# Block inverses of 16 as leading pieces in a two-layer hybrid encoder, with all projections as fill

## The chip, the cores and the metric

The kernel runs on one core of one Trainium2 chip. The metric is the device time of one execution in microseconds (us). TensorE (PE) multiplies matrices, VectorE (DVE), ScalarE (ACT) and GpSimd (POOL) work element by element, and SyncE (SP) issues most transfers. Each engine works through its own instructions in the order in which they stand in the program and waits for semaphores where it needs another engine's result.

## The reference, cut to what matters

Two layers over 512 tokens of width 1024, in float32. Each layer has a mixer and then a mixture of 16 experts:

```
xn = rmsnorm(x);  proj = xn @ w_in
y_a = gmlp_spatial_gating(a_u, a_v, ...)             # chunks of 128 tokens
y_b = dilated_attention(b_q, b_k, b_v, positions)    # 6 heads, q/k norm + rotary
y_c = gated_deltanet(c_qkv, c_gate, c_a, c_b, ...)   # 6 heads, forward and backward scan
x = x + concat(y_a, y_b, y_c) @ w_out
x = x + expert_choice_ffn(rmsnorm(x)) ; x = x + rmsnorm(p @ w_ple) * sigmoid(...)
# inside gated_deltanet, per chunk:
t_inv = triangular_solve(lower + eye, eye)           # unit lower triangular
u = t_inv @ (v * beta);  w = t_inv @ (k * beta * exp(g))
# then a scan: v_new = u - w @ state;  o = q @ state + qk @ v_new;  state = ...
```

The kernel uses chunks of 32 tokens, so it inverts 2 directions x 96 triangles of 32 x 32 per layer (24 column groups on each of 4 groups of 32 partitions, for each direction).

## The kernel before

The change is in the mixer of each layer (0 to 440 us in layer 0, 960 to 1390 us in layer 1). The experts behind it keep PE nearly full and are not touched.

The float32 products are three matmuls each (`mm3`, L345: high part by high part, low by high, high by low), so every weight is first split: `wnext` (L319) lets ACT make the rounded high part `whi` (L338) and POOL the remainder `wlo` (L340). In `mixer` (L371) the order of the code is: the projection and convolution for the DeltaNet (`gdn_qkv`; its PSUM tile is `cq`, its DVE tiles `acc` and `sl`, its transposes `tokp`), the chunks' Gram matrices (`gdn_chunk`, `pG`, `AT`), the inverse (`gdn_inv`, L883), the end of the gating (`gmlp_out`, L582: `mixp`, `ya`, `yap`), the rotary tables in layer 0, the attention's projection of q and k (`attn_qk`, L472), the transposed inverse (`gdn_inv_T`, L905), and then the scan over 16 chunks (`gdn_scan`, L915) interleaved with the rest of the attention and with the first part of the output projection.

`gdn_inv` does 30 steps on DVE, each of one product `T` (L900) and one sum into `X` (L902), over the rows below the step, for both directions at once. `gdn_inv_T` transposes `X` into `XT` by two DVE instructions and multiplies by beta (L911, L912). The first product of the scan (`pV`, L951) reads `XT`.

`attn_qk` has three groups i of 256 columns and four token tiles t. `first(i)` does 24 `mm3` matmuls into `qkp` for each t, copies and squares them on ACT, then computes the norm's factor `ra` on DVE (L183 to L190, 13 small operations), multiplies on POOL (L530) and rotates on DVE (L535 to L538). `second(i, t)` transposes the result on PE (`qkTp`, L504) and copies it on ACT into `att`. The transposes of group i are emitted behind the projections of group i + 1.

Two things set the order. The framework's scheduler places the instructions of the mixer's first part on each engine freely, by its own priorities. From the scan on `interleave` (L454) works: the scan is the lead, cut into pieces by `yield`, and the rest of the attention and the output projection (`w_out_first`) are the fill. Each lead piece yields a number, which is paid off with fill pieces; `in_order` (L435) pins the order of the pieces on PE by letting a piece issue after the last PE instruction of the piece before. The other engines are not pinned: a fill piece's work on DVE, ACT and POOL can go ahead of the lead's. `INIT` fill pieces come first; `FILLS` are the numbers that the scan yields.

Of the kernel before, what the change touches and what calls it, by code (L numbers as in the profile page):

```python
# [38 lines left out]

OWED = 0.5  # L40

INIT = 3
FILLS = (1.9, 1.5, 1.1)

QKV_BLOCKS = ((4, 5), (2, 3), (0, 1), (6, 7), (8,))
# [72 lines left out]
class K:  # L118
# [252 lines left out]
    def mixer(self, l):  # L371
        nc, tc, A = self.nc, self.tc, self.A
        with tc.tile_pool(name=f"mix{l}", bufs=1, reuse_waits="tile") as mp:
            self.mp = self.sm = mp
            self.t = lambda i, shape, name: mp.tile(shape, F32, tag=f"t{i}", name=name, bufs=2)
            self.p1 = lambda shape, name: mp.tile(shape, F32, tag="p1", name=name, bufs=3)
            self.p2 = lambda shape, name: mp.tile(shape, F32, tag="p2", name=name, bufs=2)
            self.one = lambda shape, name: mp.tile(shape, F32, tag=name, name=name, bufs=1)

            for tag, n, bufs in (("qk", 1024, 2), ("amask", S + 384, 1), ("wsT", 512, 1), ("mcst", CROUTE - CKEEP, 1),  # L380
                                 ("p1", 512, 3), ("p2", 512, 2)):
                for _ in range(bufs):
# [12 lines left out]
            specs += [(wo[0:640, c:c + n], n, 5) for c, n in WO_COLS]  # L395
            specs += [(wo[640:1024, 512 * i:512 * i + 512], 512, 3) for i in range(2)]
            self.wplan(specs)
            wuv = [self.wnext()]
            if l == 0:
                self.load_x(range(1, NT))  # L400
            xs = self.gslot("xs").rearrange("p (t d) -> p t d", t=2)
            tv = lambda name: self.slot(name).rearrange("p (k n) -> p k n", k=4)
            self.xh, self.xl = [tv("xh") for _ in range(2)], [tv("xl") for _ in range(2)]
            for t in range(NT):
                if t == 2:
                    wuv.append(self.wnext(pieces=4))
                self.norm(t, g, xs[:, t % 2, :])
                self.norm_T(t, xs[:, t % 2, :], self.xh, self.xl)
            self.setup2(l)
            self.gmlp(l, wuv)  # L410
            self.gate_decay(l)

            qkv = self.gdn_qkv(l)
            next(qkv)
            self.gdn_chunk(l)
            wq = self.wnext(ahead=False)
            next(qkv, None)
            self.gdn_inv(l)
# [12 lines left out]
            self.wo2 = [self.wnext() for _ in range(2)]  # L431
            self.gdn_out(l)
        self.w_out_last(l)

    def in_order(self):  # L435

        last = None

        def piece(gen):
            nonlocal last  # L440
            with ExitStack() as st:
# [3 lines left out]
            ins = self.nc.cur_bb.bb.instructions  # L445
            k = len(ins) - 1
            while ins[k] is not last and ins[k].engine != self.nc.tensor.engine:
                k -= 1
            last = ins[k]
            return r  # L450

        return piece

    def interleave(self, lead, fill):  # L454


        piece, owed = self.in_order(), 0.0
        for _ in range(INIT):
            piece(fill)
        while True:  # L460
            r = piece(lead)
            if r is None:
                return
            owed += r
            while owed > OWED:
                r = piece(fill)
                if r is None:
                    break
                owed -= r


    def attn_qk(self, l, wq):  # L472
# [41 lines left out]
        def first(i, w):  # L514
# [25 lines left out]

        self.wload(small=True)
        for i in range(3):
            first(i, self.wnext(small=True) if i else wq)
        self.qk_rest = lambda: second(*late.pop(0)) if late else None


# [35 lines left out]
    def gmlp_out(self, l):  # L582
# [6 lines left out]
        for j in range(2):  # L589
            self.mark("gmlp")  # L590
            ya = self.p1([128, NT, 128], "ya")
            for i in range(2):
                g = 2 * j + i
                p = self.pc([128, NT, 64], "mixp")
                pe.matmul(p, wsT[:, g, :], uv[:, :, 256 + g * 64:256 + g * 64 + 64], start=True, stop=True)
                v.scalar_tensor_tensor(ya[:, :, i * 64:(i + 1) * 64], p, bs[:, g:g + 1],
                                       uv[:, :, g * 64:(g + 1) * 64], op0=ALU.add, op1=ALU.mult)
            pt = self.pc([128, NT, 128], "yap")
            for t in range(NT):
                pe.transpose(pt[:, t, :], ya[:, t, :], self.ident)  # L600
            self.split(self.yTa[0][:, j, :], self.yTa[1][:, j, :], pt.rearrange("p t c -> p (t c)"), 0.5)

    def attn_v(self, l, wv):
        self.mark("attn_v")
        for t in range(NT):
            p = self.pb([128, 384], "vp")
            for i in range(2):
# [275 lines left out]
    def gdn_inv(self, l):  # L883
# [5 lines left out]
        v.transpose(brT, br)  # L889
        v.tensor_scalar(brT, brT, -1.0, None, op0=ALU.mult)  # L890
        X = self.gslot("X").rearrange("p (c i j) -> p c i j", c=2, i=32)
        for dr in range(2):
            Xd = X[:, dr] if dr == 0 else X[:, dr].rearrange("p i j -> p j i")
            v.transpose(Xd, AT[:, dr].rearrange("p m b -> p b m"))
            v.tensor_tensor(Xd, Xd, brT[:, dr, :, None].to_broadcast([128, 32, 32]), op=ALU.mult)
        pool_e.memset(X.rearrange("p c i j -> p c (i j)")[:, :, ::33], 1.0)
        for j in range(1, 31):
            n = 31 - j
            T = self.t(3, [128, 2, n, j], "T")
            v.tensor_tensor(T, X[:, :, j + 1:, j:j + 1].to_broadcast([128, 2, n, j]),  # L900
                            X[:, :, j:j + 1, 0:j].to_broadcast([128, 2, n, j]), op=ALU.mult)
            v.tensor_tensor(X[:, :, j + 1:, 0:j], X[:, :, j + 1:, 0:j], T, op=ALU.add)  # L902
        self.X = X

    def gdn_inv_T(self, l):  # L905
        self.mark("invT")
        v, pe, br, X = self.nc.vector, self.nc.tensor, self.br, self.X
        XT = self.XT = self.gslot("XT").rearrange("p (d m b) -> p d m b", d=2, m=32)
        for dr in range(2):
            Xd = X[:, dr] if dr == 0 else X[:, dr].rearrange("p i j -> p j i")  # L910
            v.transpose(XT[:, dr].rearrange("p m t -> p t m"), Xd)  # L911
        v.tensor_tensor(XT[:, :, 0:24], XT[:, :, 0:24], br[:, :, 0:24, None].to_broadcast([128, 2, 24, 32]), op=ALU.mult)  # L912


    def gdn_scan(self, l):  # L915
# [588 lines left out]
```

## Time and profile before

| | us |
|---|---|
| median of 3 runs | 1958.14 (1953.76 to 1958.29) |
| the profiled execution | 1962.08 |
| its span | 1960.3 |
| PE busy in the span | 1809.5 (92%) |
| DVE busy | 931.7 (48%) |
| ACT busy | 523.9 (27%) |
| POOL busy | 457.4 (23%) |

The profile is of one execution. In the windows view a row has the stretch in us, its length, and then for PE, PEld (PE's weight loads), DVE, ACT and POOL the busy time and in brackets the instructions; the last three numbers are the clock that TensorE was granted (1.00 is 2.4 GHz, 0.50 is 1.2 GHz), the share of the DMA engines and GB/s. In the timeline a row has the start, the time, the engine, the line, the operation, what it writes and reads, its tile sizes, and how many instructions were drawn together; in brackets the engine's idle time ahead of it and the instruction whose end released it. A float32 matmul or transpose through PE stands in the trace as two instructions; in the order listings below it is one. Line numbers of the kernel after are higher than those of before by up to 50.

### The profile page before, as it was taken

To read this page: it belongs to the slowest core of one execution; us is meant where nothing else is said; L and a number is where in the kernel's file an instruction comes from. 1 tells how busy PE (TensorE), PEld (TensorE's weight loads), DVE (VectorE), ACT (ScalarE), POOL (GpSimd) and SP (SyncE) were. 2 spreads that over 40 slices of the span, in tenths; PEclk is the share of its full clock that TensorE was granted. 3 is DMA by queue.
4 is the path that set the end of the run, shared out by engine and by line. 5 is a ranking of instruction groups with operands and counts; after the bars stand their busy time and mean duration, and the time that the engine had idled before them with its cause. 6 is when DMAs were issued, how large, how long until landed. Compare 5 with 4: busy or idle time off the path is not lost.

```text
span 1960.3 us, 30038 instructions
## 1 busy us (share of the span) xinstructions
PE 1809.5 (92%) x12216; PEld 1140.4 (58%) x12216; DVE 931.7 (48%) x2088; ACT 523.9 (27%) x1213; POOL 457.4 (23%) x402
## 2 busy tenths in 40 slices
PE   6898698979999999999989978899799999999999
PEld 5777665864344444434988767568544344443358
DVE  5879767671112121132778796776511212114126
ACT  4334444331010101102443344552311011011023
POOL 3544313320000003021645452233100000031025
PEclk9998788989999999999998977999799999999999
DMA  5212020187799999899342020202987999998991
GB/s 169 86 33 60 17 85 15 56 329 302 321 423 421 409 421 407 345 412 379 111 134 76 24 74 2 97 2 102 411 321 318 422 421 397 422 394 345 380 328 66
DMA packets 122394, 467.47 MB, mean 238 GB/s; under 512 B 11664, under 2 KB 68496, under 8 KB 75920
## 3 DMA queue, kind: packets, MB, share of 16 engines
q1 hardware_dynamic: 115168, 458.46, 59.5%
q10 hardware_dynamic: 7088, 7.09, 1.2%
q8 instruction: 96, 1.57, 0.3%
q14 instruction: 42, 0.34, 0.1%
HBM read 461.32 MB, written 4.19 MB: 237 GB/s over the span
## 4 chain that ended last, share of the span: by engine, by line
PE 69%; DVE 20%; ACT 3%; issue 3%; POOL 2%; DMA 2%; ACTq 0%; SPq 0%; DVEq 0%; POOLq 0%
PE pGt L1276 14%; PE pUp L1276 11%; PE pY L1276 10%; DVE acc L778 3%; PE xep L1206 2%; PE ysc L1295 2%; DVE rr L944 2%; PE xep L1207 2%; PE pY L1391 2%; PE pV L951 1%; PE op L348 1%; PE ysc L1296 1%; PE pgp L348 1%; PE pgp L350 1%; PE plep L1172 1%
## 5 line engine op out<-in xcount | busy, mean ns | idle before, releaser
L1276 PE MATMUL pGt<-w,xe 128*64 128x512 f32 x592 | 194.8, 607 | 0.0
L340 POOL TENSOR_TENSOR wlo<-w,whi 128x512 fp32r<-128x512 f32 (+5 forms) x66 | 162.1, 2473 | 102.9 <-ACT whi L338 71.9
L1276 PE MATMUL pUp<-w,xe 128*64 128x512 f32 x688 | 178.4, 593 | 0.0
L1343 POOL TENSOR_TENSOR x<-x,hh 128x1024 f32<-128x1024 f32 x8 | 18.8, 2356 | 620.0 <-DMA wx<-in_w_e_up_dram 310.4
L1276 PE MATMUL pY<-w,hidT 128*64 128x512 f32 x608 | 162.5, 596 | 0.2 <-ACT hidT L1350 0.2
L1360 DVE SCALAR_TENSOR_TENSOR yl<-pY,gsl,yh 128x512 fp32r<-128x512 f32 x28 | 21.0, 751 | 203.1 <-ACT yh L1359 201.5
L1301 DVE TENSOR_TENSOR x<-ysc,x 128x512 f32<-128x512 f32 x96 | 62.9, 686 | 110.5 <-PE ysc L1296 110.5
L1276 PEld LDWEIGHTS pUp<-w,xe 128*64 128x64 f32 x688 | 62.9, 137 | 89.5 <-issue 86.3
L1276 PEld LDWEIGHTS pGt<-w,xe 128*64 128x64 f32 x592 | 56.1, 137 | 99.2 <-issue 92.7
L1276 PE MATMUL pGt<-wx,xe 128*64 128x512 f32 x384 | 113.0, 599 | 0.3
L1334 DVE SCALAR_TENSOR_TENSOR hid<-sg,gsl,pUp 128x512 f32<-128x512 f32 x32 | 23.9, 748 | 169.8 <-PE pUp L1276 168.0
L1276 PEld LDWEIGHTS pY<-w,hidT 128*64 128x64 f32 x608 | 55.6, 136 | 76.2 <-issue 73.3
L1276 PE MATMUL pUp<-wx,xe 128*64 128x512 f32 x320 | 99.8, 595 | 0.0
L1276 PE MATMUL pY<-wx,hidT 128*64 128x512 f32 x288 | 86.2, 595 | 0.0
L1327 DVE SCALAR_TENSOR_TENSOR sg<-sg,pGt 128x512 f32<-128x512 f32 x32 | 21.7, 686 | 131.3 <-ACT sg L1326 131.3
L338 ACT ACTIVATE whi<-w 128x512 fp32r<-128x512 f32 (+5 forms) x66 | 68.2, 1058 | 38.5 <-PE op L349 15.8
L1326 ACT ACTIVATE sg<-pGt,gsl 128x512 f32<-128x512 f32 x32 | 21.8, 687 | 196.5 <-PE pGt L1276 194.6
L1350 ACT ACTIVATE hidT<-htp 128x512 f32<-128x512 f32 x32 | 19.0, 597 | 200.4 <-PE htp L1349 200.4
L1206 PE MATMUL xep<-OH,hh 128*128 128x256 f32 x256 | 70.1, 307 | 2.4 <-DVE OH L1194 2.4
L778 DVE SCALAR_TENSOR_TENSOR acc<-raw,pp,acc 128x512 f32<-128x512 f32 x72 | 64.3, 894 | 15.5 <-ACT acc L776 13.0
L348 PE MATMUL pgp<-whi,gTh 128*128 128x256 f32 x256 | 70.9, 281 | 0.0
L350 PE MATMUL pgp<-whi,gTl 128*128 128x256 f32 x256 | 69.8, 282 | 0.3 <-DVE gTl L279 0.3
(404 smaller groups left out, 4277.3 us busy)
## 6 DMA issues: line engine op xcount, KB each, us to landing
w<-in_w_e_up_dram SPq DMA_DIRECT2D x86, 1024.0 KB, 15.4
w<-in_w_e_down_dram SPq DMA_DIRECT2D x76, 1024.0 KB, 12.7
w<-in_w_e_gate_dram SPq DMA_DIRECT2D x74, 1024.0 KB, 15.6
wx<-in_w_e_gate_dram SPq DMA_DIRECT2D x48, 1024.0 KB, 9.9
wx<-in_w_e_up_dram SPq DMA_DIRECT2D x40, 1024.0 KB, 16.7
wx<-in_w_e_down_dram SPq DMA_DIRECT2D x36, 1024.0 KB, 12.0
wd<-in_w_e_down_dram SPq DMA_DIRECT2D x32, 512.0 KB, 8.3
w<-in_w_in_dram SPq DMA_DIRECT2D x14, 1024.0 KB, 5.2
```

The source lines that it names most:

```text
L338: self.nc.scalar.activation(rr_(hi[:, ks, :]), wk, AF.Copy)
L340: e.tensor_tensor(rr_(lo[:, ks, :]), wk, hi[:, ks, :], op=ALU.subtract)
L348: pe.matmul(p, lh, rh, start=first, stop=False)
L350: pe.matmul(p, ll, rh, start=False, stop=last)
L778: v.scalar_tensor_tensor(acc, raw[:, kk:kk + S], conv[:, b, kk:kk + 1], acc, op0=ALU.mult, op1=ALU.add)
L944: v.tensor_tensor(rr[kl[dr], :], vtok[kl[dr], tl, :], fl(tm[kl[dr]]), op=ALU.subtract)
L1206: pe.matmul(p, rr_(hh[:, t, ks]), OHf[:, t, :], start=(t == 0), stop=False)
L1207: pe.matmul(p, rr_(hl[:, t, ks]), OHf[:, t, :], start=False, stop=(t == NT - 1))
L1276: pe.matmul(pt[nh][64 * ei:64 * ei + 64, :], lhs[:, kk, 64 * ei:64 * ei + 64], wt[ei][k][:, nh * 512:nh * 512 + 512], start=(kk == 0), sto ...
L1295: pe.matmul(p, rr_(OT[:, t, :]), rr_(yh[:, ns]), start=True, stop=False)
L1301: v.tensor_tensor(xv, p, xv, op=ALU.add)
L1391: pe.matmul(pY[64 * ei:64 * ei + 64, :], hidT[:, 4 * half + k, 64 * ei:64 * ei + 64], wt[ei][:, k, :], start=(half + k == 0), stop=(half * ...
```

## The change

The inverse now works on four blocks of 16 x 16 (two per direction and triangle) in a new tile `XN`, by 14 steps in place of 30. The block off the diagonal of each 32 x 32 triangle comes from two products on PE: `pY1` (`AT` by `XN`) and, after a multiplication by beta on DVE (`Y`), `pY2` (`Y` by `XT`), which DVE subtracts in `XT`. ACT copies the blocks into `X`, POOL sets zeros and ones. There are two more transposes on DVE for it.

The inverse, its transposition and the scan are now one lead; the end of the gating, the projections of q, k and v, the attention and the first part of the output projection are one fill, with `yield`s added. A projection of one t and the transposes that it carries are in one piece. `in_order` also lets a fill piece's DVE, ACT and POOL instructions issue only behind the last instruction of the lead on that engine. `INIT` is 1.

```
-INIT = 3
+INIT = 1
...
-            self.gdn_inv(l)
-            self.gmlp_out(l)
-            if l == 0:
-                self.trig()
-            nc.scalar.dma_start(self.amask, A["amask"])
-            self.attn_qk(l, wq)
-            self.gdn_inv_T(l)
-            wv = [self.wnext(small=True), self.wnext()]
-
-            other = chain(self.attn_v(l, wv), self.core(l), self.w_out_first(l))
-            self.interleave(self.gdn_scan(l), other)
+
+            other = chain(self.gmlp_out(l), self.attn_qk(l, wq), self.attn_v(l), self.core(l), self.w_out_first(l))
+            self.interleave(chain(self.gdn_inv(l), self.gdn_inv_T(l), self.gdn_scan(l)), other)
...
+                if not leads:
+                    for i in ahead.values():
+                        st.enter_context(self.tc.issue_after(i))
                 r = next(gen, None)
...
+                elif leads and i.engine in (self.nc.vector.engine, self.nc.scalar.engine, self.nc.gpsimd.engine):
+                    ahead[i.engine] = i
...
-            r = piece(lead)
+            r = piece(lead, True)
...
                 if late:
                     second(*late.pop(0))
+                yield 2.6
...
+        XN = self.XN = self.one([128, 2048], "XN")
+        B = XN[:, 0:1024].rearrange("p (c e i j) -> p c e i j", c=2, e=2, i=16)
...
-        for j in range(1, 31):
-            n = 31 - j
-            T = self.t(3, [128, 2, n, j], "T")
...
+        yield 5.0
+        for j in range(1, 15):
+            n = 15 - j
+            T = self.t(3, [128, 4, n, j], "T")
+            v.tensor_tensor(T, Bf[:, :, j + 1:, j:j + 1].to_broadcast([128, 4, n, j]),
+                            Bf[:, :, j:j + 1, 0:j].to_broadcast([128, 4, n, j]), op=ALU.mult)
+            v.tensor_tensor(Bf[:, :, j + 1:, 0:j], Bf[:, :, j + 1:, 0:j], T, op=ALU.add)
+            if j % 2 == 0:
+                yield 2.6
+        for i in range(2):
+            s = slice(16 * i, 16 * i + 16)
+            act.activation(X[:, :, s, s], B[:, :, i], AF.Copy)
...
+        for dr in range(2):
+            v.transpose(flip(XN[:, dr]), flip(X[:, dr]) if dr == 0 else X[:, dr])
+        yield 6.0
+        for dr in range(2):
+            p = self.pg([128, 24, 16], "pY1")
+            for m in range(24):
+                for r in rows:
+                    pe.matmul(p[r, m, :], AT[r, dr, m, :], XN[r, dr, m, cs[dr][0]], start=True, stop=True)
+            v.tensor_tensor(Y[:, dr, :, cs[dr][0]], p, br[:, dr, 0:24, None].to_broadcast([128, 24, 16]), op=ALU.mult)
+        for dr in range(2):
+            v.transpose(flip(XT[:, dr]), X[:, dr] if dr == 0 else flip(X[:, dr]))
+        yield 5.0
+        for dr in range(2):
+            p = self.pg([128, 24, 16], "pY2")
+            for m in range(24):
+                for r in rows:
+                    pe.matmul(p[r, m, :], Y[r, dr, m, :], XT[r, dr, m, cs[dr][1]], start=True, stop=True)
+            xo = XT[:, dr, 0:24, cs[dr][1]]
+            v.tensor_tensor(xo, xo, p, op=ALU.subtract)
+            xd = XT[:, dr, 0:24]
+            v.tensor_tensor(xd, xd, br[:, dr, 0:24, None].to_broadcast([128, 24, 32]), op=ALU.mult)
+        yield 4.0
```

On PE, in layer 0, right behind the last projection of the DeltaNet (`cq`), before:

```order
L349 MATMUL cq_1350<-xl_102,whl_1113 128x512
L350 MATMUL cq_1350<-xh_100,whl_1113 128x512
L348 MATMUL qkp_1587<-whi_1301,xh_99 128x256
L349 MATMUL qkp_1587<-wlo_1302,xh_99 128x256
L350 MATMUL qkp_1587<-whi_1301,xl_101 128x256
L348 MATMUL qkp_1587<-whi_1301,xh_99 128x256
L349 MATMUL qkp_1587<-wlo_1302,xh_99 128x256
```

and after, at the same place:

```order
L349 MATMUL cq_1350<-xl_102,whl_1113 128x512
L350 MATMUL cq_1350<-xh_100,whl_1113 128x512
L807 MATMUL tokp_1389<-cst_64,sl_1342 128x128 x4
L807 MATMUL tokp_1395<-cst_64,sl_1387 128x128 x4
L596 MATMUL mixp_1407<-uv_239,wsT_237 128x256
L596 MATMUL mixp_1410<-uv_239,wsT_237 128x256
L601 MATMUL yap_1413<-cst_64,ya_1406 128x128 x4
L596 MATMUL mixp_1435<-uv_239,wsT_237 128x256
L596 MATMUL mixp_1438<-uv_239,wsT_237 128x256
L601 MATMUL yap_1441<-cst_64,ya_1434 128x128 x4
L348 MATMUL qkp_1502<-whi_1301,xh_99 128x256
L349 MATMUL qkp_1502<-wlo_1302,xh_99 128x256
```

Before, 96 matmuls `qkp` of the first group stand ahead of the second `tokp`; after, none does, and all of them stand behind the last `yap`.

The first transpose `qkTp` of q and k (`qk_1584` before, `qk_1499` after, the rotated first group), on PE in layer 0, before:

```order
L348 MATMUL qkp_1959<-whi_1938,xh_100 128x256
L349 MATMUL qkp_1959<-wlo_1939,xh_100 128x256
L350 MATMUL qkp_1959<-whi_1938,xl_102 128x256
L504 MATMUL qkTp_1788<-cst_64,qk_1584 128x128 x2
L504 MATMUL qkTp_1826<-cst_64,qk_1584 128x128 x2
L348 MATMUL qkp_1996<-whi_1938,xh_99 128x256
```

and after:

```order
L348 MATMUL qkp_1690<-whi_1669,xh_100 128x256
L349 MATMUL qkp_1690<-wlo_1670,xh_100 128x256
L350 MATMUL qkp_1690<-whi_1669,xl_102 128x256
L504 MATMUL qkTp_1721<-cst_64,qk_1499 128x128 x2
L348 MATMUL qkp_1734<-whi_1669,xh_99 128x256
L349 MATMUL qkp_1734<-wlo_1670,xh_99 128x256
```

Before, 216 matmuls `qkp` stand ahead of it: all of groups 0 and 1 and the first t of group 2; after, 120 do: group 0 and the first t of group 1. From there on a pair of transposes follows each t, so that the first pair of group 1 stands behind the first t of group 2. `pY1` stands behind the seventh pair, `pY2` behind the eighth and six `vp`.

On POOL, in the scan of layer 0 (`St` is the state's decay of one step, `o_sum` the output's sum in steps 8 to 15, `wlo` of 128x1920 and 128x1280 a low part for `w_out_first`), before:

```order
L961 TENSOR_TENSOR St<-St,ex 128x384 x5
L340 TENSOR_TENSOR wlo<-w,whi 128x1920
L961 TENSOR_TENSOR St<-St,ex 128x384 x2
L340 TENSOR_TENSOR wlo<-w,whi 128x1920
L961 TENSOR_TENSOR St<-St,ex 128x384 x2
L988 TENSOR_TENSOR o_sum<-tmp,o_sum 32x384 x2
```

and after, from the tenth step on:

```order
L1037 TENSOR_TENSOR o_sum<-tmp,o_sum 32x384 x2
L340 TENSOR_TENSOR wlo<-w,whi 128x1920
L1010 TENSOR_TENSOR St<-St,ex 128x384
L1037 TENSOR_TENSOR o_sum<-tmp,o_sum 32x384 x2
L1010 TENSOR_TENSOR St<-St,ex 128x384
L1037 TENSOR_TENSOR o_sum<-tmp,o_sum 32x384 x4
L340 TENSOR_TENSOR wlo<-w,whi 128x1920
L340 TENSOR_TENSOR wlo<-w,whi 128x1280
```

The first two low parts stood behind the decays of steps 5 and 7; now they stand behind `o_sum` of steps 11 and 14, and on PE the first output matmul that reads each of them stands right behind: behind `pV` of step 12 and behind `pO` of step 14.

## Rows read from the trace of the kernel before

**Rows 1.** Windows: the stage ahead of the scan and the scan, both layers.

```profile
154.00:228.00 74.00, 52.12 (x346) 47.90 (x344) 71.96 (x131) 37.73 (x157) 32.48 (x35) 0.82 0.19 50
...
228.00:382.00 154.00, 141.63 (x1988) 105.77 (x1989) 99.87 (x277) 61.79 (x143) 43.63 (x36) 0.89 0.11 38
...
1120.00:1196.00 76.00, 57.17 (x379) 51.65 (x377) 74.15 (x143) 37.47 (x157) 33.30 (x35) 0.80 0.19 49
1196.00:1347.00 151.00, 137.75 (x1989) 103.22 (x1990) 100.43 (x277) 62.10 (x144) 43.60 (x36) 0.92 0.12 38
```

**Rows 2.** Lines of DVE, 154 to 228: busy, mean ns, idle before.

```profile
L902 DVE TENSOR_TENSOR X<-X,T 128x60 f32<-128x60 f32 (+14 forms) x30 | 24.6, 821 | 0.4
L900 DVE TENSOR_TENSOR T<-X 128x60 f32<-128x60 f32 (+14 forms) x30 | 18.4, 613 | 0.4
...
L911 DVE STREAM_TRANSPOSE XT<-X 128x1024 f32<-128x1024 f32 x2 | 4.1, 2140 | 0.0
```

**Rows 3.** Waits of PE, 154 to 228: total us, times, longest.

```profile
PE qkTp L504 <- DVE qk L538: 11.6, 1, 11.6
```

**Rows 4.** Timeline of PE, layer 0, from `cq` to the transposes.

```profile
154.16 0.27 PE L348 MATMUL qkp<-whi,xh 128*128 128x256 f32 x1
...
168.79 0.66 PE L801 MATMUL tokp<-cst,sl 128*128 128x128 f32 x4 [2.22 <-DVE sl L783]
...
178.53 0.58 PE L349 MATMUL qkp<-wlo,xh 128*128 128x256 f32 x1 [0.96 <-POOL wlo L340]
...
195.06 0.28 PE L350 MATMUL qkp<-whi,xl 128*128 128x256 f32 x1
```

**Rows 5.** Timeline of ACT, DVE and POOL: from a projection to its rotation.

```profile
175.66 0.24 ACT L524 ACTIVATE sqa<-qk 128x64 f32<-128x64 f32 x1
...
197.79 3.95 POOL L530 TENSOR_TENSOR qk<-qk,ra 128x256 f32<-128x256 f32 x4 [9.73 <-DVE ra L190]
...
201.77 4.06 DVE L535 TENSOR_TENSOR ro<-qk,rot 128x128 f32<-128x128 f32 x4 [0.50 <-POOL qk L530]
...
215.91 2.96 POOL L530 TENSOR_TENSOR qk<-qk,ra 128x256 f32<-128x256 f32 x4 [10.22 <-DVE ra L190]
...
228.06 0.16 DVE L183 TENSOR_SCALAR nr<-ssq 128x16 f32<-128x16 f32 x1
...
230.43 0.17 DVE L190 SCALAR_TENSOR_TENSOR ra<-nr,ra 128x16 f32<-128x16 f32 x1
...
236.04 0.90 DVE L535 TENSOR_TENSOR ro<-qk,rot 128x128 f32<-128x128 f32 x4
```

**Rows 6.** Timeline of PE: small matmuls by tiles of 32.

```profile
148.15 0.77 PE L875 MATMUL pG<-KQT 64*32 64x64 f32 x48
...
361.11 0.86 PE L951 MATMUL pV<-rr,XT 32*32 32x64 f32 x24
```

**Rows 7.** Timeline of PE, DVE, POOL and ACT in the scan of layer 0.

```profile
258.48 0.85 PE L951 MATMUL pV<-rr,XT 32*32 32x64 f32 x22 [0.22 <-DVE rr L944]
...
267.26 0.85 PE L951 MATMUL pV<-rr,XT 32*32 32x64 f32 x22 [0.23 <-DVE rr L944]
...
271.89 1.81 ACT L338 ACTIVATE whi<-w 128x1920 fp32r<-128x1920 f32 x1
...
273.77 4.24 POOL L340 TENSOR_TENSOR wlo<-w,whi 128x1920 fp32r<-128x1920 f32 x1 [0.35 <-ACT whi L338]
...
275.14 3.86 DVE L944 TENSOR_TENSOR rr<-vtok,tm 32x384 f32<-32x384 f32 x2
...
279.06 1.30 PE L951 MATMUL pV<-rr,XT 32*32 32x64 f32 x22 [0.22 <-DVE rr L944]
...
299.07 5.05 DVE L944 TENSOR_TENSOR rr<-vtok,tm 32x384 f32<-32x384 f32 x2
...
316.68 0.92 PE L951 MATMUL pV<-rr,XT 32*32 32x64 f32 x24
...
321.84 2.14 POOL L988 TENSOR_TENSOR o_sum<-tmp,o_sum 32x384 f32<-32x384 f32 x2
```

More of the change, by code (lines that the diff above doesn't have):

```diff
@@ L435, in in_order, with piece @@
     def in_order(self):
-        last = None
-        def piece(gen):
+        last, ahead = None, {}
+        def piece(gen, leads=False):
             nonlocal last
+            ins = self.nc.cur_bb.bb.instructions
+            k0 = len(ins)
             with ExitStack() as st:
@@ L443, in piece @@
                     st.enter_context(self.tc.issue_after(last))
+                if not leads:
+                    for i in ahead.values():
+                        st.enter_context(self.tc.issue_after(i))
                 r = next(gen, None)
[L445 to L449, printed above, removed]
+            if ins is not self.nc.cur_bb.bb.instructions:
+                raise RuntimeError("block")
+            for i in ins[k0:]:
+                if i.engine == self.nc.tensor.engine:
+                    last = i
+                elif leads and i.engine in (self.nc.vector.engine, self.nc.scalar.engine, self.nc.gpsimd.engine):
+                    ahead[i.engine] = i
             return r
@@ L542, in attn_qk @@
         for i in range(3):
-            first(i, self.wnext(small=True) if i else wq)
+            yield from first(i, self.wnext(small=True) if i else wq)
         self.qk_rest = lambda: second(*late.pop(0)) if late else None
@@ L601, in gmlp_out, with attn_v @@
             self.split(self.yTa[0][:, j, :], self.yTa[1][:, j, :], pt.rearrange("p t c -> p (t c)"), 0.5)
-    def attn_v(self, l, wv):
+            yield 1.5
+        if l == 0:
+            self.trig()
+        self.nc.scalar.dma_start(self.amask, self.A["amask"])
+    def attn_v(self, l):
         self.mark("attn_v")
+        wv = [self.wnext(small=True), self.wnext()]
         for t in range(NT):
@@ L894, in gdn_inv @@
             v.transpose(Xd, AT[:, dr].rearrange("p m b -> p b m"))
-            v.tensor_tensor(Xd, Xd, brT[:, dr, :, None].to_broadcast([128, 32, 32]), op=ALU.mult)
-        pool_e.memset(X.rearrange("p c i j -> p c (i j)")[:, :, ::33], 1.0)
-        for j in range(1, 31):
-            n = 31 - j
-            T = self.t(3, [128, 2, n, j], "T")
-            v.tensor_tensor(T, X[:, :, j + 1:, j:j + 1].to_broadcast([128, 2, n, j]),
-                            X[:, :, j:j + 1, 0:j].to_broadcast([128, 2, n, j]), op=ALU.mult)
-            v.tensor_tensor(X[:, :, j + 1:, 0:j], X[:, :, j + 1:, 0:j], T, op=ALU.add)
+            for i in range(2):
+                s = slice(16 * i, 16 * i + 16)
+                Bd = B[:, dr, i] if dr == 0 else B[:, dr, i].rearrange("p i j -> p j i")
+                v.tensor_tensor(Bd, Xd[:, s, s], brT[:, dr, s, None].to_broadcast([128, 16, 16]), op=ALU.mult)
+        Bf = B.rearrange("p c e i j -> p (c e) i j")
+        pool_e.memset(Bf.rearrange("p c i j -> p c (i j)")[:, :, ::17], 1.0)
+        pool_e.memset(X[:, :, 0:16, 16:32], 0.0)
+        pool_e.memset(X[:, :, 16:32, 0:16], 0.0)
+        yield 5.0
[7 more added lines that the diff above has]
+                yield 2.6
+        for i in range(2):
+            s = slice(16 * i, 16 * i + 16)
+            act.activation(X[:, :, s, s], B[:, :, i], AF.Copy)
         self.X = X
@@ L906, in gdn_inv_T @@
         self.mark("invT")
-        v, pe, br, X = self.nc.vector, self.nc.tensor, self.br, self.X
+        nc = self.nc
+        v, pe, br, X, AT = nc.vector, nc.tensor, self.br, self.X, self.AT
+        rows = [slice(32 * c, 32 * c + 32) for c in range(4)]
         XT = self.XT = self.gslot("XT").rearrange("p (d m b) -> p d m b", d=2, m=32)
+        XN = self.XN.rearrange("p (d m b) -> p d m b", d=2, m=32)
+        Y = self.one([128, 2, 24, 32], "Y")
+        cs = [(slice(0, 16), slice(16, 32)), (slice(16, 32), slice(0, 16))]
         for dr in range(2):
-            Xd = X[:, dr] if dr == 0 else X[:, dr].rearrange("p i j -> p j i")
-            v.transpose(XT[:, dr].rearrange("p m t -> p t m"), Xd)
-        v.tensor_tensor(XT[:, :, 0:24], XT[:, :, 0:24], br[:, :, 0:24, None].to_broadcast([128, 2, 24, 32]), op=ALU.mult)
+            nc.gpsimd.memset(Y[:, dr, :, cs[dr][1]], 0.0)
+        flip = lambda a: a.rearrange("p i j -> p j i")
+        for dr in range(2):
[20 more added lines that the diff above has]
+        yield 4.0
     def gdn_scan(self, l):
```

## The prediction

> **What bounds the kernel now.** I read the windows first, then DVE's lines, PE's waits, and the timelines around the two places where the order changes. Each layer's mixer has two stretches that the change touches: the stage from the last `cq` to the first `pV`, and the scan. In the stage DVE is busy 71.96 of 74.00 us and PE only 52.12; in layer 1 it is 74.15 of 76 and 57.17 [rows 1]. DVE's largest part is the inverse: 24.6 + 18.4 = 43.0 us [rows 2]. So at first sight DVE sets the end of the stage, and a shorter inverse should shorten it. But what PE can do beside DVE depends on where its work stands in its queue. PE loses 11.6 us in one piece in front of the first `qkTp` [rows 3], after it has done 216 projection matmuls ahead of time. In the scan PE is the busy one: 141.63 of 154.00 us, 137.75 of 151.00 [rows 1].
>
> **The change, part by part.** All sums are for layer 0 first and on the profiled execution (1962.08 us, 3.94 above the median of 1958.14).
>
> *Start of the stage.* Before, PE fills the time from 154.16 until the second `tokp` at 168.79 with 96 `qkp` [rows 4]. After, both `tokp` come first. The second waits for `sl` on DVE, and the DVE work ahead of `sl` (the transposes of `AT`, the multiplication, the convolution's `acc`) is not what the change removes, so it comes at about 168.8 as now. PE idles from 154.2 to there, but for 0.7 us. The gating's matmuls then run as before to 177.6 (178.53 less the wait of 0.96 [rows 4]). From there 120 `qkp`: 118 took 178.53 to 195.3, or 0.142 each with the slower first ones [rows 4], so 17.1, to 194.7.
>
> *Gate 0.* The first `qkTp` needs the rotated first group, whose last projection ends after 96 of these, at 191.3. Behind it follow ACT's copy and squares (a square is 0.24 and its read as much again [rows 5]; I allow 1.4), the `ra` chain on DVE (228.06 to 230.60, 2.5 when nothing is in between), POOL's multiplication (2.96 to 3.95) and the rotation (0.90 to 4.06, plus 0.6 for its two sums) [rows 5]. That is 8.4 to 12.5, so 199.7 to 203.8; I take 203, since POOL is splitting weights as now. PE is idle for 8 us. Before, this gate was at 206.9: it comes 4 us earlier, but with 96 matmuls fewer behind it.
>
> *Gate 1.* 72 `qkp` at 0.142 and three pairs of about 0.6 are 12 us, to 215; 24 more, to 218.4. Group 1's chain of 8.4 to 12.5 from 215 ends at 223.4 to 227.5; I take 225. Another 6.6 us idle. Before, there was no such gate, since the projections ran a whole group ahead.
>
> *The block products.* 48 `qkp` and three pairs are 8.6, to 233.6. Then come 192 matmuls of `pY1`, 384 instructions in the trace. The trace has no matmul of 32 by 32 by 16 columns: the nearest are `pG` at 0.77 / 48 = 16 ns and `pV` at 0.86 / 24 = 36 ns [rows 6]. So a product is between 6.2 and 13.8 us; I take 20 ns, 7.7, nearer to `pG`, because `pV` has four times the columns. To 241.3. With 24 `qkp` and a pair, 4 us; beside them on DVE the two multiplications by beta and two transposes of 4.1 together [rows 2]; `pY2` starts at about 247 and ends at 254.7. DVE's subtraction and multiplication of both directions and the rest of `vp` put the first `pV` at about 259. The bounds, from the gates' chains and the two rates: 252 to 274.
>
> The Trainium skill, TensorEngine Tiling (Array Packing), section Instruction Overhead, gives each matmul a fixed cost of about 60 cycles, however few columns it has. At 2.4 GHz that is an estimate of 25 ns, 19 us per layer in place of my 15.4; the rows bear out that columns are not all (64 columns go at 16 and at 36 ns), and the sum would be 7 us higher for both layers.
>
> Before, the first `pV` was at 228.2 (the end of the stage [rows 1]). The stage is 31 us longer, and has done 12 `vp` and three pairs more, worth 3: **+28 in layer 0**, from 21 to 43. Layer 1 has the same order and nearly the same row [rows 1]; I take the same.
>
> What the blocks save on DVE (43.0 us become 28 operations of at most 224 elements, roughly a quarter of that) is hidden behind PE's queue and worth nothing here.
>
> *The scan, middle.* The two `wlo` of 128x1920 leave it. Beside them `rr` takes 3.86 and 5.05 us [rows 7], `pV` comes late, and PE goes on at half clock (`pV` at 1.30 in place of 0.85). Four steps from 267.26 to 316.68 take 49.4 us, against 8.78 for the one before, or about 9.0 with more fill: **−13.5** [rows 7]. Layer 1's scan is 3 us shorter now [rows 1], so I give it **−10**.
>
> The Trainium skill, SBUF, section SBUF: two separate sides, says that a VectorE operation with two SBUF inputs and a GpSimd operation that reads SBUF exclude each other for the whole instruction. The two slow `rr` beside `wlo` agree with it, and by it the last step's `rr` would wait out a `wlo` as well.
>
> *The scan, end.* The first low part now stands behind `o_sum` of step 11, its high part behind `vn` of step 12, and the output matmul that needs them right behind `pV` of step 12, ahead of `pS` and `pO`, the scan's own. PE waits for 1.81 + 4.24 [rows 7], about 6.2, and restarts at half clock, 1.5. The second stands behind `o_sum` of step 14, and nine output matmuls ahead of `pK` of step 15 wait for it: 2.14 + 4.24 and the sum ahead of it, 6.7, and 1.5 again. `rr` of step 15 meets the following `wlo`: 0 to 4, I take 2. **+18** per layer, from +8 (half hidden by fill) to +24. Fifteen output matmuls come ahead of the scan's end in place of behind it: 0 to +2.6, I take **+1.5**.
>
> *Sum.* Layer 0: 28 − 13.5 + 18 + 1.5 = +34. Layer 1: 28 − 10 + 18 + 1.5 = +37.5. Together +71.5, so the profiled execution would go from 1962.1 to 2033.6, and the median from 1958 to about **2029**. The experts behind keep their order and their time.
>
> **The rivals.**
>
> *DVE sets the end (faster).* If the gates are met (rotations done before PE reaches the transposes), the stage ends with the larger of PE's work and DVE's. DVE: 72 − 43 + 10 for 28 short operations + 7 for transposes and products = 46. PE: 52 + 15 = 67. The stage is 7 us shorter in each layer, the scan 13.5 and 10, and the waits at the end are hidden by fill: 1958 − 14 − 23.5 = about 1921. It needs the chain from a projection to its rotation to be shorter than the work between: 24 `qkp` are 3.4 us, and the least that the rows give the chain is 8.4. What speaks for it is DVE's 97% [rows 1]; against it PE's wait of 11.6 already with 216 matmuls ahead [rows 3]. It decides if the first `qkTp` waits less than 2 us.
>
> *Cheap gates, only the start lost (slower by about 1%).* The 14 us at the start stay and the products cost 15, but the idle of 11.6 before the first `qkTp` goes and the others hide: 14 + 15 − 11.6 − 3 = +14. With −13.5 and −10 in the middle and half of the wait at the end, +8: +8.5 and +12, in all about 1979.
>
> *Dear products and a longer end (slower by 5%).* Products at the rate of `pV`, 36 ns, are 27.6 per layer, 12 more; that at half clock in part, 2 more: 2029 + 28 = 2057.
>
> That the change doesn't do what it says is out: the order listings show the pieces where the code puts them.
>
> **How the numbers follow.** The forecast has 0.63, dear products 0.18, cheap gates 0.11, DVE sets the end 0.08. The range 1982 to 2062 takes in the forecast's bounds (its low bounds of stage and end are 14 + 20 below 2029, and hardly together), dear products and a part of cheap gates. A difference of under 0.3%, about 6 us, can't be told from none by such a measurement. Faster 0.08, the same 0.04 (where cheap gates meet a cheap end), slower 0.88.
>
> **What would show it.** PE idle from about 155 to 168 in layer 0, but for one group of `tokp`; two waits of `qkTp` on DVE's rotation of 5 us or more; `pY` between 16 and 36 ns; the first `pV` near 259; DVE idle for a third of the stage; `rr` at its short time in the middle of the scan; PE waiting for `wlo` twice in steps 12 and 14, about 6 us each. It is wrong if the first `pV` comes before 235, or if the scan's last four steps are no longer than the others.

## The result and the profile after

The median is 2048.09 us over 4 runs (2041.44 to 2054.96) against 1957.43 for the kernel before: a ratio of 1.0467, with a 95% interval of 1.0430 to 1.0504. The forecast was 2029, with a range of 1982 to 2062. The span of the profiled execution went from 1960.3 to 2046.5 us, by 86.2.

Windows of the kernel after, cut at its own first `pV` and last `pO`: the stage and the scan of layer 0, then of layer 1.

```profile
154.00:264.00 110.00, 67.42 (x1126) 62.79 (x1127) 54.13 (x137) 41.97 (x167) 36.57 (x54) 0.72 0.14 35
264.00:415.00 151.00, 130.76 (x1988) 97.42 (x1988) 92.32 (x258) 61.59 (x140) 40.72 (x32) 0.95 0.13 43
1164.00:1273.00 109.00, 68.65 (x1126) 63.84 (x1127) 53.20 (x127) 40.68 (x166) 38.61 (x54) 0.73 0.14 35
1273.00:1425.00 152.00, 132.44 (x1974) 99.02 (x1974) 91.83 (x258) 59.95 (x137) 40.70 (x32) 0.93 0.12 41
```

Beside [rows 1]: the stage grew from 74 and 76 us to 110 and 109, although DVE has 18 us less to do in layer 0 and is now busy for half of it. PE is busy for 67 of 110 us, at a mean clock of 0.72. No engine is full any more: the stage is a chain that passes from PE to ACT, DVE, POOL, DVE and back to PE. The scan kept its length.

What PE waits for from 150 to 275 us of the kernel after (total us, times, longest), in place of the one wait of [rows 3]:

```profile
PE qkTp L504 <- DVE qk L539: 17.3, 2, 8.9
PE tokp L807 <- DVE sl L789: 11.6, 2, 7.1
PE pY L956 <- issue: 4.6, 2, 2.6
PE pY L947 <- issue: 4.2, 2, 2.6
```

The timeline of PE in the same stretch, to be laid beside [rows 4]:

```profile
161.01 1.12 PE L807 MATMUL tokp<-cst,sl 128*128 128x128 f32 x4 [7.11 <-DVE sl L789]
...
166.62 1.12 PE L807 MATMUL tokp<-cst,sl 128*128 128x128 f32 x4 [4.50 <-DVE sl L789]
...
203.33 0.66 PE L504 MATMUL qkTp<-cst,qk 128*128 128x128 f32 x2 [8.94 <-DVE qk L539]
...
225.84 0.66 PE L504 MATMUL qkTp<-cst,qk 128*128 128x128 f32 x2 [8.39 <-DVE qk L539]
...
234.56 1.73 PE L947 MATMUL pY<-XN,AT 32*32 32x16 f32 x185
238.88 1.90 PE L947 MATMUL pY<-XN,AT 32*32 32x16 f32 x128 [2.60 <-issue]
242.34 1.16 PE L947 MATMUL pY<-XN,AT 32*32 32x16 f32 x71 [1.55 <-issue]
...
249.72 1.46 PE L956 MATMUL pY<-XT,Y 32*32 32x16 f32 x152
...
264.87 0.86 PE L1000 MATMUL pV<-vtok,XT 32*32 32x64 f32 x24
```

The reader is to see the order's three prices: idle time in front of both `tokp`, where 96 `qkp` stood; two gates in front of the first `qkTp` of groups 0 and 1, at 203.3 and 225.8; and the products from 234.6 to 243.5 and again from 249.7.

At the scan's end, PE and POOL in the steps 12 and 14 of the kernel after:

```profile
376.97 0.69 PE L349 MATMUL op<-wlo,yTa 128*128 128x384 f32 x1 [3.92 <-POOL wlo L340]
...
404.91 0.69 PE L349 MATMUL op<-wlo,yTa 128*128 128x384 f32 x1 [6.47 <-POOL wlo L340]
...
372.69 4.23 POOL L340 TENSOR_TENSOR wlo<-w,whi 128x1920 fp32r<-128x1920 f32 x1 [6.08 <-issue]
...
400.63 10.67 POOL L340 TENSOR_TENSOR wlo<-w,whi 128x1920 fp32r<-128x1920 f32 x3
```

Both output matmuls that read a fresh low part wait for it with the scan's own work queued behind them. From the first instruction of `pV` in step 12 to that in step 15 it is 43.0 us in layer 0; it was 25.8. The twelve steps ahead of them go from 123.0 to 104.0 us: no `rr` is late there any more (a pair takes 1.09 to 1.14 us).

### The profile page after: what moved, and what is told of

Read it like the earlier page. It is cut to its first block, busy times and chain, and to the rows that moved or that the text cites. A ratio compares the mean times of both kernels' runs of the same rounds, so it can differ in the third digit from the quotient of the medians.

```text
span 2046.5 us, 33071 instructions
## 1 busy us (share of the span) xinstructions
PE 1822.7 (89%) x13752; PEld 1159.3 (57%) x13752; DVE 880.5 (43%) x2042; ACT 527.1 (26%) x1217; POOL 455.5 (22%) x410
## 5 line engine op out<-in xcount | busy, mean ns | idle before, releaser
L1325 PEld LDWEIGHTS pUp<-w,xe 128*64 128x64 f32 x688 | 62.6, 137 | 88.8 <-issue 86.2
L1325 PE MATMUL pY<-wx,hidT 128*64 128x512 f32 x288 | 86.2, 595 | 0.0
L349 PE MATMUL pgp<-wlo,gTh 128*128 128x256 f32 x256 | 72.4, 286 | 0.3 <-POOL wlo L340 0.3
## 6 DMA issues: line engine op xcount, KB each, us to landing
w<-in_w_e_up_dram SPq DMA_DIRECT2D x86, 1024.0 KB, 15.7
wx<-in_w_e_up_dram SPq DMA_DIRECT2D x40, 1024.0 KB, 17.3
```

The lines of the kernel that those rows point to most:

```text
L349: pe.matmul(p, lh, rl, start=False, stop=False)
L1325: pe.matmul(pt[nh][64 * ei:64 * ei + 64, :], lhs[:, kk, 64 * ei:64 * ei + 64], wt[ei][k][:, nh * 512:nh * 512 + 512], start=(kk == 0), sto ...
```

## The experiments

**Blocks alone.** The body of the inverse and its products as in the change; the order as before.

```
-            other = chain(self.gmlp_out(l), self.attn_qk(l, wq), self.attn_v(l), ...)
-            self.interleave(chain(self.gdn_inv(l), self.gdn_inv_T(l), self.gdn_scan(l)), other)
+            run = lambda g: [None for _ in g]
+            run(self.gdn_inv(l)); run(self.gmlp_out(l)); run(self.attn_qk(l, wq)); run(self.gdn_inv_T(l))
+            wv = [self.wnext(small=True), self.wnext()]
+            other = chain(self.attn_v(l, wv), self.core(l), self.w_out_first(l))
+            self.interleave(self.gdn_scan(l), other)          # INIT = 3, no hold on DVE, ACT, POOL
```

> The block inverse with its products alone; the order of the kernel before (free placing of the inverse, the gating and the projections, three fill pieces first, nothing held on DVE, ACT or POOL). Theory (the order costs, the blocks cost little): DVE's 43 us of steps become about 10, the wait of 11.6 us before the first qkTp shrinks to under 4, the products cost about 18 us of PE per layer with their waits for instructions, so the first pV of layer 0 comes at 225 to 238 with 24 vp more done, the scan is as before; time 1945 to 1970 us. Rival (the block products are what makes the changed kernel slow): 1990 us or more. Rival (DVE set the end): under 1935 us.

Measured 1968.88 us, ratio 1.0053 (1.0034 to 1.0073). So of the 91 us, 80 are what the order costs once the blocks are in. In the window of this kernel's stage DVE is busy for 68% in place of 97 and PE for 78% in place of 70. Counted from the start of the last `cq` to the first `pV`, the stage takes 78.1 us in layer 0 and 81.2 in layer 1, where it took 74.3 and 74.0, with the products in it. The wait at the first `qkTp` is gone in layer 0; PE waits 5.8 us for the inverse's transpose `XN` in front of `pY1` instead. The window of layer 0:

```profile
155.00:234.00 79.00, 61.26 (x1121) 56.02 (x1119) 53.49 (x128) 39.94 (x164) 32.74 (x41) 0.86 0.18 48
```

**The order alone.** The change's order with the 30 steps on DVE and no products on PE.

```
-        for j in range(1, 15):              # four blocks of 16
+        for j in range(1, 31):              # two of 32, as before
+            if j % 4 == 0:
+                yield 2.6
```

> The order of the changed kernel (inverse as lead, gating, q, k, v and attention as fill, fill held behind the lead on all engines), with the inverse of 30 steps on DVE and no products on PE. Theory: gates and late start stay (two waits of qkTp of 7 us or more each, PE idle from 154 to 167), 18 us of products per layer go, the longer inverse on DVE makes the first gate later by up to 10 us: 2010 to 2045 us. Rival (the block products are what makes the changed kernel slow): 1960 to 1975 us.

Measured 2025.03 us, ratio 1.0340 (1.0305 to 1.0376): the order alone makes the kernel 67 us slower. The waits of PE from 150 to 270 show a longer first gate:

```profile
PE qkTp L504 <- DVE qk L539: 28.0, 2, 19.6
```

The timeline of DVE, with PE's gate at its end, shows why. The squares of the first group are done at 195.98, but the operations of `ra` and the rotation come only between the last steps of the longer inverse:

```profile
203.88 0.17 DVE L183 TENSOR_SCALAR nr<-ssq 128x16 f32<-128x16 f32 x1
...
213.42 0.22 DVE L907 TENSOR_TENSOR T<-X 128x60 f32<-128x60 f32 x1
213.56 0.89 DVE L536 TENSOR_TENSOR ro<-qk,rot 128x128 f32<-128x128 f32 x4
...
215.13 0.66 PE L504 MATMUL qkTp<-cst,qk 128*128 128x128 f32 x2 [19.57 <-DVE qk L539]
```

The two experiments do not add up to 91: the order alone costs 67 us and the blocks alone 11, but in the new order the blocks cost 23. The shorter inverse does help there: the first gate opens at 203.3 in place of 215.1. The stretch with the products then takes more than that back, and the first `pV` comes at 264.9 in place of 256.7.

**No hold.** The change without its rule for DVE, ACT and POOL.

```
-                if not leads:
-                    for i in ahead.values():
-                        st.enter_context(self.tc.issue_after(i))
```

> The changed kernel without the rule that a fill piece's instructions on DVE, ACT and POOL issue only behind the lead's; the order of pieces on PE stays. Theory: the two waits of PE for wlo at the scan's end (3.9 and 6.5 us, with the stretched steps of 16.7 and 18.2 us) go, about 18 us per layer, and two slow rr beside wlo in mid-scan come back, 10 to 14 us: 2030 to 2045 us. Rival (the hold is most of the loss): under 2000 us.

Measured 2015.47 us, ratio 1.0290 (1.0258 to 1.0323): 33 us less than the kernel after, between the two readings. The steps 12 to 15 take 26.2 us in layer 0 in place of 43.0. The stage ahead of the scan is as long as with the hold. From the first `pV` to the last router matmul `pl` it is 13 us shorter in layer 0 and 20 in layer 1. The expectation had the slow `rr` back, and that was wrong: the low parts are in mid-scan again, but in this order they fall between two `rr`, as POOL's and DVE's timelines of this kernel show:

```profile
327.48 4.24 POOL L340 TENSOR_TENSOR wlo<-w,whi 128x1920 fp32r<-128x1920 f32 x1 [6.08 <-ACT vn L1001]
...
335.82 1.13 DVE L990 TENSOR_TENSOR rr<-vtok,tm 32x384 f32<-32x384 f32 x2
```

So the hold costs about what it was forecast to, 18 per layer at the scan's end, and most of what it gives in mid-scan another placing gives too: steps 4 to 8 of layer 0 take 39.1 us here, 33.1 in the kernel after and 49.9 before. The stretch behind the scan is shorter as well: from the last `pO` to the last `pl` it is 48.3 and 46.9 us before, 50.5 and 55.1 after, 45.4 and 47.0 here.

**Projections ahead of the gating.** In the change's fill.

```
-            other = chain(self.gmlp_out(l), self.attn_qk(l, wq), self.attn_v(l), ...)
+            other = chain(self.attn_qk(l, wq), self.gmlp_out(l), self.attn_v(l), ...)
```

> The changed kernel with the projections of q and k ahead of the end of the gating in the fill (the rotary tables are made ahead of both). Theory: the 11.6 us of PE idle for sl before the two tokp are filled with qkp, as before the change, the gates behind stay: about 12 us less per layer, 2015 to 2035 us. Rival (PE's idle start was hidden by DVE anyway): 2040 us or more.

Measured 2043.31 us, ratio 1.0428 (1.0394 to 1.0463). The rival holds: it is 5 us less, not 25, and the runs of the two kernels overlap. The stages got hardly shorter: from the start of the last `cq` to the first `pV`, both layers together take 221.3 us, where they took 221.9. The idle time moved into the first gate, in the timelines of POOL, DVE and PE of this kernel:

```profile
189.16 2.55 POOL L533 TENSOR_TENSOR qk<-qk,ra 128x256 f32<-128x256 f32 x4 [2.94 <-DVE ra L190]
...
193.67 3.67 DVE L941 STREAM_TRANSPOSE XN<-X 128x1024 f32<-128x1024 f32 x2 [1.33 <-ACT X L923]
197.20 0.85 DVE L538 TENSOR_TENSOR ro<-qk,rot 128x128 f32<-128x128 f32 x4
...
198.73 0.66 PE L506 MATMUL qkTp<-cst,qk 128*128 128x128 f32 x2 [18.92 <-DVE qk L541]
```

Counted from the last `cq` (158.6 here, 153.9 in the kernel after) the projections begin 24 us earlier, but the first gate opens only 9 us earlier, at 40 for 49, and the first `pV` of layer 0 comes 3.5 us earlier; in layer 1 it comes 2.8 later. POOL is done at 191.7, and the rotation stands behind the lead's two transposes on DVE, which wait for ACT's copies of the finished blocks. The waits say the same: 11.6 us for `sl` are gone, the gates' 17.3 are 25.6, and the gating's `yap`, now between the products, waits 3.7.

**Low parts in pieces, in the kernel before.** This tests the term of mid-scan by itself.

```
-            wh, wl = self.wnext()
+            wh, wl = self.wnext(pieces=5)          # in w_out_first
```

> The kernel before, with the high and low parts of the first output weights made in five pieces of 384 or 256 columns (one per 128 rows) instead of one instruction of up to 1920. Theory (rr waits out the whole low part beside it): rr waits for one piece of about 0.9 us at most, the four long steps of 11.8 to 13 us become about 9, in both layers: 1935 to 1948 us. Rival (those steps are long because of their fill): 1953 to 1962 us.

Measured 1936.31 us, ratio 0.9898 (0.9880 to 0.9916): faster than both kernels. The four steps that took 49.4 us take 35.3. POOL's and DVE's timelines of this kernel, beside [rows 7]:

```profile
273.60 5.46 POOL L340 TENSOR_TENSOR wlo<-w,whi 128x384 fp32r<-128x384 f32 x5
...
275.36 1.88 DVE L944 TENSOR_TENSOR rr<-vtok,tm 32x384 f32<-32x384 f32 x2
```

The two `rr` beside the pieces take 1.88 us, where they took 3.86 beside one whole low part of 4.24, although all pieces together are longer.

**Later transposes, in the kernel after.**

```
-                if late:
+                if late and t >= 2:
                     second(*late.pop(0))
+                    second(*late.pop(0))
```

> The changed kernel with the transposes of a group of q and k two pairs at a time behind the third and fourth projection of the next group, so that 48 more qkp (6.8 us) stand ahead of each gate; nothing else moves. Theory (the two gates cost 17 us of PE's time per layer because too little stands ahead of them): each wait falls from 8.9 and 8.4 us to about 2, 27 us for both layers: 2015 to 2030 us. Rival (the idle time moves to the block products or pV): 2038 us or more.

Measured 2019.94 us, ratio 1.0324 (1.0302 to 1.0347): 28 us less, as the theory of the gates had it. The waits of PE, where it was 17.3 in two:

```profile
PE qkTp L504 <- DVE qk L540: 6.6, 2, 3.3
```

**Blocks without products, in the order of before.** Each set of 96 small matmuls is one matmul of 384 columns through the identity, so the block off the diagonal is left out.

```
-            for m in range(24):
-                for r in rows:
-                    pe.matmul(p[r, m, :], AT[r, dr, m, :], XN[r, dr, m, cs[dr][0]], start=True, stop=True)
+            pe.matmul(p, self.ident, AT[:, dr, 0:24, cs[dr][0]], start=True, stop=True)
```

> The blocks in the order of before (the first experiment), with each set of 96 small products replaced by one matmul of 384 columns through the identity; the block off the diagonal is therefore not computed. Theory (384 small matmuls cost PE about 18 us per layer, waits for instructions among them, which eats what DVE saves): 1930 to 1945 us, under the kernel before. Rival (PE had that time free; the loss of the first experiment lies elsewhere): 1960 us or more.

Measured 1944.58 us, ratio 0.9940 (0.9917 to 0.9964). The products cost 24.3 us of the first experiment's 1968.9, 12.2 per layer. Without them the shorter inverse gains 0.6%: that is all that DVE's relief is worth here, since PE's own work is 53.92 us of this stage's 71, with gates between:

```profile
158.00:229.00 71.00, 53.92 (x357) 48.83 (x355) 50.61 (x109) 38.05 (x154) 29.03 (x36) 0.86 0.20 53
```

**Three together, in the kernel after:** no hold, the later transposes, and the pieces.

```
-                    for i in ahead.values():
-                        st.enter_context(self.tc.issue_after(i))
...
+                if late and t >= 2:
+                    second(*late.pop(0))
...
+            wh, wl = self.wnext(pieces=5)
```

> Three undone at once in the changed kernel: no hold on DVE, ACT and POOL, the later transposes, and output weights split in pieces of 384 columns. Theory (separate costs that add): 33 us for the hold, 27 for the gates, 0 to 8 for the pieces: 1980 to 1992 us, still slower than before by the late start and the products. Rival (they overlap): 2000 us or more.

Measured 1984.97 us, ratio 1.0144 (1.0115 to 1.0173): the costs add, as expected.

**And the projections ahead of the gating.**

```
+            other = chain(self.attn_qk(l, wq), self.gmlp_out(l), self.attn_v(l), ...)   # on top of the three
```

> The previous experiment's kernel (no hold, later transposes, output weights in pieces) and the projections of q and k ahead of the end of the gating in the fill. With both gates short, filling the start should pay now. Theory (the fourth experiment gained little because the first rotation stood behind the lead's transposes on DVE and the idle time only moved into the first gate): 11 us per layer, 1960 to 1973 us. Rival (the start's idle time is not on the path): 1980 us or more.

Measured 1976.47 us, ratio 1.0085 (1.0052 to 1.0117): 8.5 us, less than half of what the theory gave. None of it is in the stages, which take 195.2 us in both layers together and took 195.1 in the previous experiment. Between the two layers, where this edit changes nothing, 5.6 us went. The first gate is still there, 40 us behind the last `cq` (161.5) as in the fourth experiment, and the rotation still stands behind the lead's transposes, in the timelines of DVE and PE:

```profile
196.71 3.68 DVE L939 STREAM_TRANSPOSE XN<-X 128x1024 f32<-128x1024 f32 x2 [1.33 <-ACT X L921]
200.26 0.85 DVE L536 TENSOR_TENSOR ro<-qk,rot 128x128 f32<-128x128 f32 x4
...
201.78 1.09 PE L503 MATMUL qkTp<-cst,qk 128*128 128x128 f32 x4 [11.71 <-DVE qk L539]
```

**All output weights in pieces, in the kernel before.**

```
-            self.wo2 = [self.wnext() for _ in range(2)]
+            self.wo2 = [self.wnext(pieces=3) for _ in range(2)]
```

> The kernel before with the first output weights in five pieces, and the last two output weights in three pieces each too. Theory: the last steps meet at most one piece, a gain of 0 to 4 us on 1936: 1931 to 1938 us. Rival (more ACT and POOL instructions at the scan's end delay vn or o_sum): 1939 us or more.

Measured 1936.49 us, ratio 0.9887 (0.9863 to 0.9911): no difference from five pieces in the first part alone.

**The blocks and the pieces, in the order of before.**

```
+            self.interleave(self.gdn_scan(l), other)          # blocks in the order of before
...
+            wh, wl = self.wnext(pieces=5)
```

> The block inverse with its products in the order of before, with the first output weights in five pieces. Theory (the two effects add: +10 us for the blocks, -20 for the pieces): 1943 to 1953 us, slower than the pieces alone. Rival (the blocks pay once the scan is clean): under 1935 us.

Measured 1945.63 us, ratio 0.9929 (0.9903 to 0.9956). The blocks cost 9 us on the better kernel as they cost 11 on the one before.

## Why the prediction was right, step by step

**The direction and the cause.** The order makes the kernel slower: 67 us alone, 80 with the blocks in. The blocks are the smaller part, 11 us in the old order and 23 in the new: the first two experiments show it from both sides. Undone one after the other, starting at 2048: the hold 33 us, gates and long low parts 30, the projections ahead of the gating 8, the rest of the pieces' order 31 (1976.5 to 1945.6), the blocks 9; against the 1957 of before, the long low parts in mid-scan give 20 back.

**The start.** The forecast had `tokp` at 168.8 and the gating's end at 177.6; they came at 166.6 and 177.9. But its place in the sum was too simple. That PE stands still there is seen; that it costs 11 us per layer is not, since filling it took 0.6 us off the two stages together in the fourth experiment and nothing in the ninth. The forecast did not see what comes next once the start is filled: the rotation is queued behind the lead's transposes on DVE, and in both experiments the first gate opened 40 us behind the last `cq`, where it had been 49 in the kernel after.

**The gates.** Forecast at 203 and 225 with 8 and 6.6 us idle; measured at 203.3 and 225.8 with 8.9 and 8.4. The chain from a projection to its rotation was worked out from [rows 5], and 48 `qkp` more ahead of each gate took 28 us off the kernel. That the first gate came out to the half microsecond is partly luck. Its last projection ended at 191.5 (forecast 191.3), but ACT needed until 194.8 (3.3 us for 1.4), since it made `whi` in between, and `ra` took 4.4 us for 2.5, since its first two operations took 1.06 and 1.19 us while POOL made `wlo`, and 0.17 each at the second gate. POOL's multiplication and the rotation, forecast at 4.5 to 8.6 us together, took 3.8. In the timelines of DVE and POOL after:

```profile
194.88 1.06 DVE L183 TENSOR_SCALAR nr<-ssq 128x16 f32<-128x16 f32 x1 [5.62 <-ACT sqa L524]
...
199.40 2.33 POOL L531 TENSOR_TENSOR qk<-qk,ra 128x256 f32<-128x256 f32 x4 [2.28 <-DVE ra L190]
```

**The products.** Forecast at 7.7 us each and 15.4 per layer; 8.9 and 9.1 from the first to the last in the trace after, 12.2 by the experiment that takes them out of the old order. The rate of 20 ns an instruction was near the mean of 23 (8.9 us by 384) for a reason that it did not give: the instructions follow each other at 12 ns in the mean (4.8 us by 384 in the first product, 4.5 in the second), and in between PE stands for 1.5 to 2.6 us on "issue". By the Trainium skill's page TensorEngine Tiling (Array Packing), section Instruction Overhead, the prediction had an estimate of 25 ns for each instruction at 2.4 GHz, 19 us per layer. The trace does not agree: at the granted clock of 1.00 an instruction took 9.4 ns (1.73 us by 185), and so a float32 matmul, which is two, 18.7. That the 19 us are near the 18.0 from first to last is due to the waits.

**The first `pV`.** Forecast at 259, measured at 264.9. Of the 6 us, 4 had come by the end of the second product (258.8 for 254.7), and 2 are in the `vp` and the two pairs behind it. Counted from the last `cq`, the stage grew by 37.1 us in layer 0 and by 36.5 in layer 1.

**The scan.** In the middle −19.0 us from step 0 to 12 in layer 0 (forecast: −13.5, and −3 for pairs and `vp` done before) and −15.0 in layer 1 (forecast −10 and −3); at the end +17.2 and +18.5 (forecast +18). The output matmuls ahead of the scan's end, forecast at +1.5, added nothing: from the last `pV` to the last `pO` it is 1.6 us less in layer 0. Both waits of PE for `wlo` came where they were forecast (3.9 and 6.5 us for 6.2 and 6.7), the two `rr` of step 15 took 3.01 and 3.05 us in the two layers beside the following `wlo`, 1.9 above the usual 1.13 (forecast 2), and the fifth experiment shows the term of mid-scan by itself.

**What the sum missed.** 71.5 forecast, 86.2 measured in the span. The two stages grew by 73.6 us for 62. The two scans went from +9.5 forecast, with the 3 us per layer for pairs and `vp` taken from them, to −1.5. These two misses, 11.6 and −11.0, cancel, and that is luck. What is left of the difference lies where nothing was forecast, in the two places below; the two ends of the program make −1.6.

Behind the scan, from the last `pO` to the last `pl`, it is 2.2 and 8.2 us more. PE has the same work there at a lower clock, in the windows behind the last `pO` of layer 0, in the kernel after:

```profile
415.00:460.00 45.00, 39.51 (x230) 34.56 (x224) 28.38 (x83) 11.36 (x21) 6.67 (x7) 0.92 0.61 229
```

Before, in 382 to 423, it was busy for 39.08 of 41 us at a clock of 1.00. Part of it is one wait: the first `pl` needs the router's weights `wr`, which POOL multiplies as soon as their transfer has landed, as POOL and PE show in layer 0 of the kernel after:

```profile
447.70 0.41 POOL L1123 TENSOR_TENSOR wr<-wr,pp 128x128 f32<-128x128 f32 x1 [21.70 <-DMA wr<-in_w_router_dram]
...
448.15 1.06 PE L1151 MATMUL pl<-wr,xT 128*128 128x16 f32 x8 [1.87 <-POOL wr L1123]
```

The transfer took 14.4 and 15.7 us from issue to landing in the two layers, where it took 2.3 before and 4.5 and 6.1 without the hold; PE waited for it for 1.9 and 3.1 us in the kernel after and not at all in the other two. The hold is not the whole cause, since the stretch is short too (47.5 and 45.8 us) with the hold and the projections ahead of the gating. Why the transfer is slow is not shown.

Between the layers it is 5.3 us more, with PE busy for as long (664.8 us for 664.9). Two of its waits for DVE account for it, in the waits from 466 to 1163.9 of the kernel after:

```profile
PE ysc L1344 <- DVE x L1350: 3.4, 2, 2.5
PE pgp L350 <- DVE gTl L279: 3.1, 2, 2.9
```

Before, `ysc` waited 1.2 us and `pgp` did not wait. All kernels here in the old order are like the one before, and all in the new order have both waits (`pgp` 1.9 to 3.9 us), but for the ninth experiment, which has neither. That is most of the 5.6 us which that experiment gained between the layers. Why DVE is late there, in code that the change does not touch, is not shown.

**The rivals.** "DVE sets the end" has its share only where the order is the old one and the products are left out, and there it is worth 0.6%. "Cheap gates" is refuted by 17.3 us of waits and the 28 us that the later transposes bring. "Dear products" had the total nearly right, at 2057, for a wrong reason: it had 36 ns an instruction, and the mean was 23 with the waits.

**Left open.** With the hold, the gates, the start and the long low parts undone, the fixed order still costs 31 us over the free one. Its first `pV` comes 96.7 and 98.5 us after the start of the last `cq` in the two layers, where the free placing with the same blocks takes 80 in both, and its first gate still waits 11.7 us for the rotation behind the inverse. Taking the rotation ahead of the lead's transposes was not tried.

## What to carry to other kernels

An engine that is 97% busy in a stage need not be what sets its end: ask, for each wait in the other engines' queues, how much work stands ahead of it, and whether the new order keeps that much. Here an order pinned on the engine that has the work, and held on the engines that prepare it, turned the making of the output weights into waits; letting the preparation go ahead took 33 us off. A wait that is seen is not yet time to be gained: filling the idle start moved it to the next gate, which another queue held. Where a long element-wise instruction on one engine stands beside a short one on the critical path, cut the long one in pieces: one argument (`pieces=5`) gave 1% here.

## What the runs showed of the hardware

PE did not take the small matmuls in one stream: 384 instructions of 32 by 32 by 16 columns came in groups, of which those in the middle have 128, with 1.5 to 2.6 us on "issue" in between. In a group they came at 9.4 and 9.6 ns each while the granted clock was 1.00 and at 15 to 16 ns at 0.50, in the windows of the first two groups of `pY1` in the kernel after:

```profile
234.60:236.30 1.70, 1.68 (x186) 1.58 (x185) 0.00 (x0) 1.67 (x9) 0.00 (x0) 1.00 0.00 0
...
238.90:240.80 1.90, 1.89 (x128) 1.78 (x128) 0.56 (x1) 0.00 (x0) 0.00 (x0) 0.50 0.03 9
```

The profiles list 108 packets on the DMA queue q8, of the kind "instruction", in the kernels with the products and 96 in those without, which fits a wait for instructions but does not prove it.

DVE and POOL held each other up on `rr` and `wlo`: a pair of `rr` took 3.86 us beside a low part of 4.24 us, 1.88 beside pieces of about 1.1, and 1.13 alone. This agrees with the Trainium skill, SBUF — State Buffer, section SBUF: two separate sides, by which a VectorE operation with two inputs in SBUF and a GpSimd operation that reads SBUF exclude each other for the whole instruction. What was not expected is that it depends on a placing by a few microseconds: in the kernel without the hold the same low parts in mid-scan met no `rr` at all.
